# Sixteen weight slots, each at its own remainder modulo 256 bytes

## The chip, the core and the metric

One core of one Trainium2 chip runs the whole kernel. The metric is the device time of one execution in microseconds; the median of the runs shown counts. Five engines matter: TensorE (PE, and its weight loads PEld), VectorE (DVE), ScalarE (ACT), GpSimd (POOL) and the queue of SyncE (SP) that issues most DMAs. SBUF is the on-chip memory of 128 partitions; an address below is a byte offset within a partition, and a tile of 512 float32 columns takes 2048 bytes of each.

## The reference

One decoder block on x of 1024 rows by 1024 columns, float32:

```python
h    = rms_norm(x, norm1_g)
proj = h @ w_in                      # 1024 x 3584: retention q,k,v,gate; differential q,k,v
ret  = rms_norm(retention_chunkwise(rotary(rq), rotary(rk), rv)) * silu(rg)   # 8 heads of 64
dif  = rms_norm((softmax(q1 k1') - lam * softmax(q2 k2')) v) * (1 - LAMBDA_INIT)  # 4 heads of 128, causal
x    = x + concat([ret, dif]) @ w_out
h2   = rms_norm(x, norm2_g)
x    = x + (silu(h2 @ w_gate) * (h2 @ w_up)) @ w_down     # 2816 wide
```

## The kernel before

**Three matmuls for one.** Every large product is made to float32 accuracy from the faster type float32r: each operand is split into a high part (a rounded copy, made by ScalarE, or by a scaled activation) and a low part (the operand minus its high part, by VectorE). `mm3` then issues high-high, high-low and low-high into the same PSUM bank. So TensorE runs triples of matmuls, 512 columns wide (384 in the differential head groups), each with its own load of a stationary block of 128 columns (512 bytes).

**The weight slots.** The pool `wp` holds eight slots for high parts (tag `whi`), eight for low parts (tag `wlo`) and two raw pages (`raw`), in that order. A slot is a tile of 512 float32r columns. The list `slot` names the first eight pairs, which the planned part of the kernel reuses by hand; later, `Strassen.weights` and `operand` take new tiles of the same two tags, which the pool hands out in turn over the same places. The slots hold, in order of time:

- in the differential stage (0 to about 235 us) the 384 columns of w_in of head groups 0 and 2 (`w_chunk`, `w_parts`), streamed against stationary blocks of the transposed x (`hT`). Groups 1 and 3 use `dslot`, another pool on the right side of SBUF with tags of the same names, which the change does not touch;
- in the seven products P1 to P7 of the retention projection, twice (to about 470 us), the weights (`prepare`, `halves_`, `product`), streamed against `hT`, `sx` and `sb`;
- in the output projection (`o_proj`) the transposed mixture as stationary blocks (`mix_turn`), and in its second half four of w_out's blocks as streams (`wo_part`);
- in the gate and up products (about 555 to 950 us), seven products for each pair of column blocks, weights as stationary blocks (`first_weights`, `Strassen.weights`), with the normalised x (`blk`, tiles elsewhere) streamed;
- in the down product (950 us to the end) both sides: `operand` makes the slot pair of an activation block (stationary) and the next pair for the weights (streamed).

**What lies where.** On the left side of SBUF the constants come first, then the pools `act`, `wp`, `st`, `rowa` and those opened later (`dif`, `sx`, `sbp`, `ap`); on the right `edge` (one tile of 24 columns that nothing reads), `wd`, later `prp`. Behind the constants and `edge`, rows of tiles are multiples of 256 bytes.

**Order.** Up to the gate and up products the instructions are planned: each is added with an engine, an estimated duration and the names of what it reads and writes (`Plan.add`), the plan assigns times (`Plan.times`), and the instructions are issued in that order. From there on the loops issue them in program order. Neither looks at an address. Two lines make and hand out the slots:

```python
    slot = [[wp.tile([P, 512], F32R, tag=tag, name=tag) for tag in ("whi", "wlo")] for _ in range(KC)]
    ...
        hi, lo = (wp.tile([P, 512], F32R, tag=tag_, name=tag_) for tag_ in ("whi", "wlo"))
```

Of the kernel before, what the change touches and what calls it, by code (L numbers as in the profile page):

```python
# [11 lines left out]
F32R = mybir.dt.float32r  # L12
# [4 lines left out]
P = 128  # L17
# [3 lines left out]
KC = D // P  # L21
# [9 lines left out]
NP = 5  # L31
NAT = 4
WARM = 2


C_ID = 0
# [36 lines left out]
def block_kernel(ctx: ExitStack, tc: tile.TileContext, x, norm1_g, w_in, ret_norm_g, dq_g, dk_g,  # L73
# [39 lines left out]
    wp = ctx.enter_context(tc.tile_pool(name="wp", bufs=KC))  # L113
# [190 lines left out]

    late = {}
    hT = [[act.tile([P, 4, 2, 4, P], F32R, tag="act", name="act") for _ in range(2)] for _ in range(2)]
    slot = [[wp.tile([P, 512], F32R, tag=tag, name=tag) for tag in ("whi", "wlo")] for _ in range(KC)]
    rawk = [(f"raw{i}", wp.tile([P, 512], F32, tag="raw", name="raw", bufs=NRAW)) for i in range(2)]
    mixd = [rowa.tile([P, 512], F32, tag="rowa", name="rowa") for _ in range(NT)]
    rowk = [(f"ra{i}", mixd[i]) for i in range(NT)]  # L310
# [54 lines left out]
    V.memset(zero, 0.0)  # L365
    for _ in range(WARM):
        T.matmul(bank[0], zero[:, :P], zero, start=True, stop=True)
# [383 lines left out]
    for s in range(ND + 3):  # L751
# [10 lines left out]
        if s < ND:  # L762
            g, k = s // NT + 1, s % NT
# [654 lines left out]
    class Strassen:  # L1418
# [10 lines left out]
        def weights(self, n):  # L1429
            (i, j), other, op, *_ = PRODUCTS[n]  # L1430
            src = self.raw[j][:, :, i, :]
            if other is not None:
                both = wp.tile([P, 512], F32, tag="raw", name="sum", bufs=NRAW).rearrange("p (k e) -> p k e", e=P)
                G.tensor_tensor(out=both, in0=src, in1=self.raw[other[1]][:, :, other[0], :], op=op)
                src = both
            hi, lo = (wp.tile([P, 512], F32R, tag=tag_, name=tag_).rearrange("p (k e) -> p k e", e=P)
                      for tag_ in ("whi", "wlo"))
            A.copy(hi, src)
            self.w[n] = hi, lo
            V.tensor_tensor(out=lo, in0=src, in1=hi.bitcast(F32), op=ALU.subtract)  # L1440
# [45 lines left out]
    at = {}  # L1486
# [42 lines left out]


    def operand(x_, y_=None, op=None):
        hi, lo = (wp.tile([P, 512], F32R, tag=tag_, name=tag_) for tag_ in ("whi", "wlo"))
        if y_ is not None:
            both = wp.tile([P, 512], F32, tag="raw", name="sum", bufs=NRAW)
            G.tensor_tensor(out=both, in0=x_, in1=y_, op=op)
            x_ = both
        A.copy(hi, x_)
        V.tensor_tensor(out=lo, in0=x_, in1=hi.bitcast(F32), op=ALU.subtract)
        return hi, lo
# [3 lines left out]
    for n, (_, (b0, b1, bop), outs, done) in enumerate(DOWN):  # L1543
        m = [bankh() for _ in range(4)] if n % 2 == 0 else [bankp(), bankp(), bankm([P, 512]), bankm([P, 512])]
        for c in range(NH):
            b = [w_get(c, *name) for name in (b0, b1) if name is not None]
            i = n * NH + c
            ah, al = operand(ring[i % len(ring)])
            if i + len(ring) < 7 * NH:
                a_load(i + len(ring))  # L1550
            bh, bl = operand(*b, bop) if bop else operand(*b)
            if i in LAST:
                plane(LAST[i], NH - 1)

            if n < len(STARTS) and c < 4:
                for sh, dh in STARTS[n]:
                    t = 4 * sh + c
                    acc[t][dh] = (rowa if dh else prp).tile([P, 512], F32, tag="rowa" if dh else "pr", name="acc")
                    SY.dma_start(acc[t][dh], x2d[t * P:(t + 1) * P, dh * 512:(dh + 1) * 512])
            for t in range(4):  # L1560
                mm3(m[t], ah[:, t * P:(t + 1) * P], al[:, t * P:(t + 1) * P], bh, bl, c == 0, c == NH - 1)
        for t in range(4):
            for (sh, dh), sign in outs.items():
                o = acc[4 * sh + t][dh]
                V.tensor_tensor(out=o, in0=o, in1=m[t], op=ALU.add if sign > 0 else ALU.subtract)
                if (sh, dh) in done:
                    row = (4 * sh + t) * P
                    SY.dma_start(out[0, row:row + P, dh * 512:(dh + 1) * 512], o)
# [25 lines left out]
```

## Time and profile before

| what | before |
|---|---|
| median of 2 runs (lowest, highest) | 1180.64 us (1179.64, 1181.64) |
| profiled execution: its own time, its span | 1179.49 us, 1177.7 us |
| granted TensorE clock, mean | 0.999 |
| PE busy | 1169.5 us, 5872 matmuls |
| PE weight loads busy | 1004.7 us |
| DVE, ACT, POOL busy | 895.4, 604.5, 506.5 us |
| matmuls of 512 columns that read a slot, mean duration of one | 389 to 401 ns |

The profile is of one execution, whose own time is 1.8 us longer than the span from its first to its last instruction. All instructions of this kernel are recorded under one line of the source (a helper's, L101), so groups are told apart by the names of the tiles they write and read, out<-in, with buffer numbers left out. Durations of matmuls overlap (one of 512 columns lasts 389 ns while the next starts after some 227 ns), so the pace is read from start to start.

### The profile page before, as it was taken

The page shows a single profiled execution, that of the slowest core. Times are in us where ns is not written, and L with a number is a line of the kernel's source. Part 1 is how long each engine was busy: PE and PEld are TensorE (multiplying, and loading weights), DVE is VectorE, ACT ScalarE, POOL GpSimd, SP SyncE. Part 2 cuts the span into 40 slices and gives each one's busy share as a digit, 9 for nine tenths or more (in the row PEclk, how much of TensorE's full clock was granted, in tenths as well). Part 3 has the DMA queues.
Part 4 walks back from the last instruction along what each step waited for, and adds up shares of the span by engine and source line. Part 5 has one row for each costly group of instructions (what it writes and reads, how often), then busy time and mean ns, then how long its engine had stood idle before and what let it go on. Part 6 is the DMA issues. An engine that isn't in the chain of part 4 may idle for free.

```text
span 1177.7 us, 17427 instructions
## 1 busy us (share of the span) xinstructions
PE 1169.5 (99%) x5872; PEld 1004.7 (85%) x5872; DVE 895.4 (76%) x1561; ACT 604.5 (51%) x1332; POOL 506.5 (43%) x581
## 2 busy tenths in 40 slices
PE   9999999999999999999999999999999999999998
PEld 7999999988888888888888888888888888888887
DVE  6988888888779866758987756666665769698696
ACT  7767566666366745836444343434344334344442
POOL 4668786510012111301276654565456535263153
PEclk9999999999999999999999999999999999999999
DMA  7278776537644862322133423332323388933341
GB/s 213 69 173 150 136 115 117 162 124 235 223 126 148 266 201 90 95 88 90 58 131 117 134 76 98 111 119 90 99 99 116 106 293 265 354 101 90 98 138 67
DMA packets 118009, 164.29 MB, mean 139 GB/s; under 512 B 11936, under 2 KB 62240, under 8 KB 117792
## 3 DMA queue, kind: packets, MB, share of 16 engines
q1 hardware_dynamic: 110976, 152.62, 39.4%
q0 software_dynamic: 5760, 10.49, 6.5%
q8 instruction: 46, 0.75, 0.3%
q14 instruction: 43, 0.35, 0.1%
q10 hardware_dynamic: 1184, 0.07, 0.1%
HBM read 110.97 MB, written 54.26 MB: 140 GB/s over the span
## 4 chain that ended last, share of the span: by engine, by line
PE 93%; DVE 4%; ACT 2%; issue 1%; DMA 1%; SPq 0%; POOL 0%; DVEq 0%; ACTq 0%
PE h L101 39%; PE pp L101 31%; PE m L101 19%; PE big L101 4%; ACT pr L101 1%; DVE wx L101 1%; DVE wy L101 1%; DVE wlo L101 1%; DMA spare<-in_w_in_dram 1%; DVE pr L101 0%; DVE rowa L101 0%; DVE sx L101 0%; ACT wy L101 0%; DVE acc L101 0%; ACT whi L101 0%
## 5 line engine op out<-in xcount | busy, mean ns | idle before, releaser
L101 POOL TENSOR_TENSOR sum<-rawp 128x512 f32<-128x512 f32 x100 | 141.8, 1419 | 175.0 <-DVE wlo L101 144.9
L101 ACT CAST whi<-sum 128x512 fp32r<-128x512 f32 x155 | 96.4, 622 | 197.8 <-PE h L101 58.7
L101 DVE TENSOR_TENSOR wlo<-sum,whi 128x512 fp32r<-128x512 f32 x155 | 158.6, 1024 | 34.4 <-ACT whi L101 34.2
L101 PE MATMUL pp<-whi,act 128*128 128x384 f32 (+1 forms) x592 | 180.9, 359 | 0.2 <-DVE qkn L101 0.2
L101 POOL TENSOR_TENSOR sum<-wide 128x512 f32<-128x512 f32 x55 | 85.7, 1560 | 128.5 <-DVE wlo L101 101.8
L101 PEld LDWEIGHTS pp<-whi,act 128*128 128x128 f32 x592 | 109.4, 188 | 4.9 <-ACT q L101 0.6
L101 PE MATMUL h<-sx,whi 128*128 128x512 f32 x360 | 111.3, 390 | 0.0
L101 DVE TENSOR_TENSOR wlo<-wide,whi 128x512 fp32r<-128x512 f32 x99 | 77.5, 805 | 33.2 <-ACT whi L101 33.2
L101 ACT CAST whi<-wide 128x512 fp32r<-128x512 f32 x99 | 59.3, 621 | 84.2 <-PE m L101 43.3
L101 PE MATMUL pp<-wlo,act 128*128 128x384 f32 (+1 forms) x296 | 102.5, 346 | 0.0
L101 PEld LDWEIGHTS h<-sx,whi 128*128 128x128 f32 x360 | 67.2, 188 | 13.7
L101 DVE TENSOR_TENSOR wlo<-rawp,whi 128x512 fp32r<-128x512 f32 x44 | 48.6, 1105 | 38.6 <-ACT whi L101 37.7
L101 PE MATMUL h<-whi 128*128 128x512 f32 x196 | 76.7, 391 | 0.0
L101 DVE TENSOR_TENSOR c<-c,h 128x512 f32<-128x512 f32 x80 | 52.9, 681 | 31.3 <-PE h L101 31.3
L101 PE MATMUL h<-whi,wlo 128*128 128x512 f32 x196 | 76.3, 389 | 0.0
L101 PE MATMUL h<-wlo,whi 128*128 128x512 f32 x196 | 76.3, 389 | 0.0
L101 POOL TENSOR_TENSOR fsum<-c 128x512 f32<-128x512 f32 x50 | 70.7, 1426 | 8.1 <-DMA ffd<-fsum 8.1
L101 PE MATMUL h<-sx,wlo 128*128 128x512 f32 x180 | 70.1, 389 | 0.0
L101 POOL TENSOR_TENSOR stt<-stt,cs 128x1 f32<-128x1 f32 (+1 forms) x64 | 57.9, 906 | 3.7
L101 PEld LDWEIGHTS pp<-wlo,act 128*128 128x128 f32 x296 | 55.9, 189 | 1.9
L101 DVE CUSTOM_DVE_ANT_0 big<-big,zm 128x128 f32<-128x128 f32 (+7 forms) x64 | 47.7, 771 | 8.8 <-PE big L101 8.6
L101 PE MATMUL h<-b,whi 128*128 128x512 f32 x176 | 54.3, 390 | 0.0
(328 smaller groups left out, 3136.4 us busy)
## 6 DMA issues: line engine op xcount, KB each, us to landing
wide<-ffd SPq DMA_DIRECT2D x77, 256.0 KB, 2.7
ffd<-fsum SPq DMA_DIRECT2D x55, 256.0 KB, 2.0
rawp<-in_w_gate_dram SPq DMA_DIRECT2D x22, 512.0 KB, 3.5
rawp<-in_w_up_dram SPq DMA_DIRECT2D x22, 512.0 KB, 3.6
wide<-in_w_down_dram SPq DMA_DIRECT2D x44, 256.0 KB, 5.4
sumd<-act POOLq DMA_DIRECT2D x40, 256.0 KB, 4.2
rowa<-cd SPq DMA_DIRECT2D x32, 256.0 KB, 2.9
cd<-pr SPq DMA_DIRECT2D x24, 256.0 KB, 2.8
```

The source lines that it names most:

```text
L101: i = getattr(self.engine, op)(*(now(a) for a in args), **{k: now(a) for k, a in kw.items()})
```

## The change

The row of a slot's tile grows from 512 to 520 elements (2080 bytes, which is 8 x 256 + 32), and the slot is a view of 512 of them: from the first element on for high parts, from the fifth (16 bytes on) for low parts. So the eight slots of each tag lie 32 bytes apart modulo 256, and all sixteen begin at different remainders. The three places that took such tiles now take the view. Instructions, their shapes and their order stay.

```diff
+SKEW = {"whi": 0, "wlo": 4}
...
-    slot = [[wp.tile([P, 512], F32R, tag=tag, name=tag) for tag in ("whi", "wlo")] for _ in range(KC)]
+    def spaced(tag):
+        at = SKEW[tag]
+        return wp.tile([P, 520], F32R, tag=tag, name=tag)[:, at:at + 512]
+
+    slot = [[spaced(tag) for tag in ("whi", "wlo")] for _ in range(KC)]
...
-            hi, lo = (wp.tile([P, 512], F32R, tag=tag_, name=tag_).rearrange("p (k e) -> p k e", e=P)
+            hi, lo = (spaced(tag_).rearrange("p (k e) -> p k e", e=P)
                       for tag_ in ("whi", "wlo"))
...
-        hi, lo = (wp.tile([P, 512], F32R, tag=tag_, name=tag_) for tag_ in ("whi", "wlo"))
+        hi, lo = (spaced(tag_) for tag_ in ("whi", "wlo"))
```

## The prediction

> **What bounds the kernel now.** I read the page's share of engines and its chain first, then the same span cut by stage.
>
> ```profile
> PE 1169.5 (99%) x5872; PEld 1004.7 (85%) x5872; DVE 895.4 (76%) x1561; ACT 604.5 (51%) x1332; POOL 506.5 (43%) x581
> ...
> PE 93%; DVE 4%; ACT 2%; issue 1%; DMA 1%; SPq 0%; POOL 0%; DVEq 0%; ACTq 0%
> ```
>
> TensorE is busy for 99% of the span and holds 93% of the chain that ended last. Only something that changes TensorE's pace, or starves it, can move the time. The stages say the same:
>
> ```profile
> 0.00:235.00 235.00, 231.92 (x1476) 221.64 (x1477) 193.28 (x544) 159.40 (x442) 154.24 (x287) 1.00 0.64 142
> 235.00:470.00 235.00, 234.56 (x1204) 198.80 (x1202) 186.72 (x331) 137.85 (x316) 29.74 (x53) 1.00 0.54 176
> 470.00:560.00 90.00, 89.38 (x491) 76.46 (x491) 63.34 (x108) 57.43 (x146) 17.58 (x32) 1.00 0.29 92
> 560.00:950.00 390.00, 390.00 (x1723) 322.92 (x1722) 266.65 (x367) 158.94 (x274) 210.62 (x150) 1.00 0.31 104
> 950.00:1178.00 228.00, 223.65 (x987) 184.87 (x985) 185.39 (x214) 90.85 (x156) 94.34 (x60) 1.00 0.53 178
> ```
>
> The columns are the stretch, its length, then busy time with count for PE, weight loads, VectorE, ScalarE and GpSimd, the granted clock and the DMA share. The clock is 1.00 throughout, so it is no lever. From 560 us on, TensorE is covered almost without a hole; VectorE, next in line, has 228.0 - 185.4 = 42.6 us free in the last stage.
>
> A matmul's "busy" is modelled, so the pace has to come from start to start. The chain in order of time gives it (start, length, what, how many matmuls):
>
> ```profile
> 33.11 3.13 PE pp L101 x18
> ...
> 261.20 5.44 PE h L101 x24
> ...
> 1083.89 29.92 PE h L101 x132
> ```
>
> 5.44 / 24 and 29.92 / 132 are both 226.7 ns for a matmul of 512 columns. At 33 us they are 384 columns wide: 3.13 / 18 = 173.9 ns. So 128 columns cost 52.8 ns, 0.4125 ns each, and 512 columns would be 211.2 ns: **about 15.5 ns of each matmul do not depend on its width**. That the pace is so even, whatever VectorE, ScalarE and the DMAs are doing, is the most useful fact here: accesses of other engines to the weight slots do not reach TensorE.
>
> It is not even everywhere. Just after a break (transposes, waits) the starts are uneven for a while:
>
> ```profile
> 243.78 0.40 PE L101 MATMUL big<-kl,qz 128*128 128x512 f32 x1
> 244.01 0.40 PE L101 MATMUL big<-kh,q 128*128 128x512 f32 x1
> 244.25 0.39 PE L101 MATMUL big<-kl,qz 128*128 128x512 f32 x1
> 244.47 0.39 PE L101 MATMUL big<-kh,q 128*128 128x512 f32 x1
> 244.70 0.40 PE L101 MATMUL big<-kl,qz 128*128 128x512 f32 x1
> 244.94 0.39 PE L101 MATMUL big<-kh,q 128*128 128x512 f32 x1
> 245.16 0.39 PE L101 MATMUL big<-kl,qz 128*128 128x512 f32 x1
> ```
>
> The steps are 0.23, 0.24, 0.22, 0.23, 0.24, 0.22: between about 220 and 240 ns, in the mean (245.16 - 243.78) / 6 = 230 ns, with no semaphore to wait for between them. The same matmuls then settle at 226.7 ns and stay. So the pace depends on some phase between the streams that TensorE reads, and in long runs it finds one that repeats. This is where an address could matter.
>
> **The change, part by part.** No instruction, DMA, wait or queue position is added, removed or moved: the hand-written order comes from names and estimated durations, which the addresses do not enter. What moves are addresses. Before, the tiles behind the constants have rows that are multiples of 256 bytes, so all operands of the wide matmuls have one remainder modulo 256. After it, slot i of the eight stands 32 i bytes further, and the low parts 16 more: sixteen slots, sixteen remainders. Each pool of eight slots grows by 8 x 32 = 256 bytes, so what lies behind keeps its remainder, and nothing else changes its place against the others.
>
> How many matmuls read a slot? The tile views of the two names, cut by stage, give 528 + 550 + 230 + 1149 + 966 = 3423 with a high part and 264 + 281 + 125 + 574 + 637 = 1881 with a low part:
>
> ```profile
> 0.00:235.00 235.00, 158.23 (x528) 97.27 (x528) 24.97 (x40) 25.04 (x40) 1.00 0.64 142
> 235.00:470.00 235.00, 176.18 (x550) 102.66 (x550) 41.64 (x60) 38.36 (x60) 1.00 0.54 176
> 470.00:560.00 90.00, 65.58 (x230) 41.01 (x231) 12.15 (x18) 11.18 (x19) 1.00 0.29 92
> 560.00:950.00 390.00, 352.95 (x1149) 215.37 (x1148) 128.20 (x144) 88.65 (x143) 1.00 0.31 104
> 950.00:1178.00 228.00, 222.30 (x966) 180.93 (x964) 149.72 (x154) 89.76 (x154) 1.00 0.53 178
> ```
>
> ```profile
> 0.00:235.00 235.00, 89.30 (x264) 49.93 (x264) 24.97 (x40) 1.00 0.64 142
> 235.00:470.00 235.00, 107.57 (x281) 52.87 (x281) 41.64 (x60) 1.00 0.54 176
> 470.00:560.00 90.00, 44.08 (x125) 23.51 (x125) 12.15 (x18) 1.00 0.29 92
> 560.00:950.00 390.00, 223.19 (x574) 107.55 (x574) 128.20 (x144) 1.00 0.31 104
> 950.00:1178.00 228.00, 197.72 (x637) 119.55 (x637) 149.72 (x154) 1.00 0.53 178
> ```
>
> Those that read one of each are counted twice:
>
> ```profile
> L101 PE MATMUL h<-whi,wlo 128*128 128x512 f32 x196 | 76.3, 389 | 0.0
> L101 PE MATMUL h<-wlo,whi 128*128 128x512 f32 x196 | 76.3, 389 | 0.0
> ...
> L101 PE MATMUL pp<-wlo,whi 128*128 128x512 f32 x78 | 30.3, 389 | 0.0
> ...
> L101 PE MATMUL pp<-whi,wlo 128*128 128x512 f32 x78 | 30.3, 389 | 0.0
> ...
> L101 PE MATMUL m<-wlo,whi 128*128 128x512 f32 x66 | 25.7, 389 | 0.0
> L101 PE MATMUL m<-whi,wlo 128*128 128x512 f32 x66 | 25.7, 389 | 0.0
> ```
>
> 2 x (196 + 78 + 66) = 680. Of the rest, two head groups (1 and 3) read slots of another pool under the same names, 2 x 8 x 8 x 3 = 384. That leaves 3423 + 1881 - 680 - 384 = **4240 matmuls** of 5872 whose reads move, nearly all of them 512 wide. Each nanosecond per matmul is 4.2 us.
>
> The cost of one moved read is not in the trace: every wide matmul had the same remainder. It is bounded by the steps above. From below: the shortest, about 224 ns within the 10 ns that the rows resolve, 2.7 less than the settled 226.7: -11 us; and, if the whole width-independent part could vanish, -15.5 x 4240 = -66 us. From above: the longest, about 236 ns, at every one of them: +9.3 x 4240 = +39 us. **I take nothing**, which is nearest to the rows: the pace of the last three stages is the same for matmuls that load slots (560 to 950 us, where the slots are the stationary or moving side of all) and for those that stream them, and the same for 384 and 512 columns but for the width.
>
> The Trainium skill ("SBUF — State Buffer", section "Who interferes with whom") speaks against any effect: TensorE has a read port each for the streamed operand and for weight loads, and waits on nobody. By that rule the sum is exactly 0. The trace agrees for other engines (the even 226.7 ns) but its uneven steps after breaks show that TensorE's own pace is not one constant, and no run so far has two remainders to compare.
>
> Writes and reads of the slots by ScalarE and VectorE:
>
> ```profile
> L101 ACT CAST whi<-sum x155: 603/623/627, 576.6 to 1163.9; 128x512 fp32r<-128x512 f32 x155
> L101 DVE TENSOR_TENSOR wlo<-sum,whi x155: 675/691/1787, 581.3 to 1164.9; 128x512 fp32r<-128x512 f32 x155
> ```
>
> Minimum, median and maximum. ScalarE's spread is 24 ns; VectorE's long ones coincide with GpSimd at work and have nothing to do with a remainder that all shared. If a shifted slot cost each 24 ns, that would be about 300 x 24 = 7 us on each engine, beside TensorE, which is not waiting for them: in the six rows of two slots above its idle time is 0.0. If that cover went, TensorE would wait for low parts in the last stage, where VectorE has those 42.6 us free. I cost it at 0.
>
> The sum: 1179.49 (the profiled execution, span 1177.7 and 1.8 around it) + 0 = 1179.5; the median of the two runs is 1.2 above that, so **1180.6**, with 4 us either way for runs and small shifts.
>
> **The rivals.**
>
> 1. *The repeat is lost* (other side: slower). If the phase that long runs settle in depends on equal remainders, the three matmuls of a triple (high-high, high-low, low-high) now follow each other with unequal ones and the pace stays that of the uneven stretches. Price: 230 - 226.7 = 3.3 ns, 14 us at all 4240 and 7 us at half; with 20 ns of rounding in the 1.38 us it may be 19 us. Time 1187 to 1199. It decides from the first long run, at 257 us; earlier, transposes break the runs anyway. For it: the steps of 220 to 240 ns without a wait. Against it: a phase may belong to when instructions are issued, not to where they read.
> 2. *The new remainders collide.* As 1, but most matmuls take the longest step: 24 to 39 us, 1204 to 1220. For it: such steps exist. Against: in the rows they alternate with short ones.
> 3. *A better phase*, the short steps more often than now: 3 to 11 us less, 1169 to 1177.
> 4. *Equal remainders are what costs the 15.5 ns.* All operands begin on one remainder, so weight load and stream could get in each other's way at every matmul, and spreading them would end it. Between a third and all of 66 us: 1114 to 1157; TensorE would then stand at about 213 us in the last stage, still above VectorE's 185. For it: the fixed part is there and unexplained. Against: a collision of two streams would hardly cost the same at 384 and 512 columns. The Trainium skill ("TensorE: Matmul & The Clock Gate", section "Wait — 56ns, not 53.3ns?") has 215.7 ns for 512 warm columns, measured back to back; by that 11.0 ns of the 226.7 are excess, 47 us over these matmuls, an estimate that gives 1134. The trace does not show that pace for any wide matmul of this kind.
> 5. *The change does not do what it says*: if rows of 520 elements were rounded up, the spacing would vanish and only the 16 bytes remain. It ends like my forecast and is held in it.
>
> **How the numbers follow.** Forecast 0.44 (1176 to 1185), rival 1 0.26, rival 3 0.10, rival 2 0.12, rival 4 0.08. Within 2% of 1180.6 lie 1157 to 1204 (2% is about what a measurement of this kernel can tell from no change): the first three cases, 0.80; faster 0.08; slower 0.12. The range of 1168 to 1200 takes in the forecast, rival 1 and rival 3.
>
> **What would show it.** The chain's groups of 24 matmuls stay at 5.44 us if I am right; 5.5 or more is rival 1, 5.6 and up rival 2, 5.4 and less rival 3 or 4. The stretch from 560 to 950 us, where the slots meet tiles that did not move, and the last one, where both sides are slots, should then differ, since their remainders do. I am wrong if these groups change; if they do not but the time does, it is a wait of TensorE for a low part, and the idle time before those six groups would be above zero.

## The result, and the profile after

The changed kernel takes 1199.39 us (1198.34 to 1200.44), against 1180.64 before: 18.75 us more, a ratio of 1.0163 with a 95% interval of 1.0146 to 1.0180. That is the upper end of rival 1 (1187 to 1199), not the forecast of no change.

The page of the changed kernel (its profiled span is 1198.6 us), the same parts as before:

```profile
PE 1190.5 (99%) x5872; PEld 1007.0 (84%) x5872; DVE 886.8 (74%) x1561; ACT 605.1 (50%) x1332; POOL 507.7 (42%) x581
...
PE 95%; DVE 2%; ACT 2%; DMA 0%; issue 0%; POOL 0%; SPq 0%; DVEq 0%; ACTq 0%
```

The counts are the same, the clock too, and the other engines' busy time is within 9 us of what it was. TensorE holds more of the chain, and the 21 us are all in its own row: it is busy longer with the same matmuls. The chain in order of time says where (start, length, what, how many matmuls). Before:

```profile
257.10 4.09 PE pp L101 x18
...
561.65 10.88 PE h L101 x48
...
964.21 29.92 PE h L101 x132
...
1143.73 27.89 PE h L101 x123
```

and after:

```profile
34.84 3.15 PE pp L102 x18
...
259.25 4.19 PE pp L102 x18
263.44 5.56 PE h L102 x24
...
567.82 11.16 PE h L102 x48
...
980.51 30.58 PE h L102 x132
...
1164.00 28.50 PE h L102 x123
```

The four rows of before are the same matmuls as those at 259.25, 567.82, 980.51 and 1164.00 us after. The delay is 2.15 us at the first, 6.17 at the second, 16.30 at the third and 20.88 at the end of the last (1192.50 against 1171.62). So the long runs of wide matmuls pay: 4.0 us in the retention products and the output projection, 10.1 in the gate and up products, 4.6 in the down product. The differential stage pays next to nothing by its pace (3.15 / 18 = 175 ns, 173.9 before: 0.02 us in this group). Of its 2.15 us, 1.73 stand before the first row (34.84 against 33.11), and a kernel below, with everything moved together, shows the same delay without any loss of time. A group of 48 takes 232.5 ns each in place of 226.7, one of 132 takes 231.7.

The two-slot groups and the writers of the slots, in the views shown before:

```profile
L102 PE MATMUL h<-whi,wlo 128*128 128x512 f32 x196 | 77.3, 394 | 0.0
L102 PE MATMUL h<-wlo,whi 128*128 128x512 f32 x196 | 76.8, 392 | 0.0
```

```profile
L102 ACT CAST whi<-sum x155: 602/622/627, 582.9 to 1183.8; 128x512 fp32r<-128x512 f32 x155
L102 DVE TENSOR_TENSOR wlo<-sum,whi x155: 677/686/1789, 588.0 to 1184.8; 128x512 fp32r<-128x512 f32 x155
```

TensorE does not wait before these groups (0.0), their mean duration is 3 to 5 ns up from 389, and the engines that write the slots take as long as before (medians of 622 and 686 ns, 623 and 691 before). What remains is the pace of TensorE with nobody in its way.

### The profile page after: what moved, and what is told of

It reads as the page before. It is cut to its first block, busy times and chain, and to the rows that moved or that the text cites. A ratio compares the mean times of both kernels' runs of the same rounds, so it can differ in the third digit from the quotient of the medians.

```text
span 1198.6 us, 17427 instructions
## 1 busy us (share of the span) xinstructions
PE 1190.5 (99%) x5872; PEld 1007.0 (84%) x5872; DVE 886.8 (74%) x1561; ACT 605.1 (50%) x1332; POOL 507.7 (42%) x581
## 4 chain that ended last, share of the span: by engine, by line
PE 95%; DVE 2%; ACT 2%; DMA 0%; issue 0%; POOL 0%; SPq 0%; DVEq 0%; ACTq 0%
PE h L102 40%; PE pp L102 32%; PE m L102 19%; PE big L102 4%; ACT pr L102 1%; ACT wy L102 0%; DMA rowa<-cd 0%; DVE wlo L102 0%; DVE wx L102 0%; POOL stt L102 0%; DVE acc L102 0%; ACT whi L102 0%; DVE wy L102 0%; DVE pr L102 0%; SPq L102 0%
## 5 line engine op out<-in xcount | busy, mean ns | idle before, releaser
L102 DVE TENSOR_TENSOR wlo<-sum,whi 128x512 fp32r<-128x512 f32 x155 | 149.4, 964 | 34.7 <-ACT whi L102 34.4
```

What stands on the lines that cost most here:

```text
L102: i = getattr(self.engine, op)(*(now(a) for a in args), **{k: now(a) for k, a in kw.items()})
```

## The experiments

Four theories stood for why. **A**: a run of matmuls settles (its steps from start to start become even) only while those that follow each other begin at equal remainders. **B**: it is the distance modulo 256 between the stationary and the streamed operand that costs. **C**: only the 16 bytes matter. **D**: only the old remainder itself is fast. In the changed kernel and in the first four experiments every engine issues the same instructions with the same waits as before; the sweeps and the last two kernels differ in some waits, so there the pace of unbroken stretches is read and not the time.

### One half of the change at a time, and one common shift

```diff
-SKEW = {"whi": 0, "wlo": 4}
+SKEW = {"whi": 0, "wlo": 0}          # spacing only, rows of 520
```

> Rows of 520 elements, but low parts not shifted: the eight slots of a tag lie 32 bytes apart modulo 256, the high and low part of a pair are equal. Theory A (lost repeat: the pace settles only while the matmuls that follow each other have operands at the same remainders): within the 12 matmuls of a gate or up product all slot operands are equal and only the next product starts elsewhere, so part of the settling comes back: 1186 to 1195 us, groups of 12 in the gate and up stage between 2.72 and 2.79 us. Theory B (a certain distance between stationary and streamed operand costs, whatever comes before): the seven of eight slots that are away from the streamed tiles stay slow, 1196 to 1200 us. Theory C (only the 16-byte shift of low parts matters): back to 1181 us.

Measured: 1200.15 us, ratio 1.0163 (1.0148 to 1.0178). The expectation was wrong on one point of fact: in the down product the pool hands out slots in the order in which they come free, so high and low parts of a pair are often not neighbours and their remainders differ there. In the gate and up stage they are equal, and there it can be read.

```diff
     # rows of 512, low slots 32 bytes on
+    his = [wp.tile([P, 512], F32R, tag="whi", ...) for _ in range(KC)]
+    wp.tile([P, 8], F32R, tag="pad1", ...)
     ... the eight "wlo" tiles
+    wp.tile([P, 56], F32R, tag="pad2", ...)
```

> Rows of 512 elements as before; all low slots 32 bytes further on, high slots where they were, pages behind in place. Only two remainders. Theory A: high and low follow each other in every triple, so the repeat is broken everywhere the slots are used: 1192 to 1200 us, unless a pattern of three repeats by itself, which would show as one fixed length for all groups of 24 matmuls. Theory B: only the third of the matmuls that load or stream a low part is slow: +5.4 ns at some 1400, 1187 to 1190 us. Theory C: 1181 if only distances that are no multiple of 32 matter.

Measured: 1201.84 us, ratio 1.0178 (1.0161 to 1.0195). That is just beyond A's 1192 to 1200 and far from B's 1187 to 1190: moving the low slots alone costs as much as the whole change. The sweep of the low parts, below, comes back to this.

```diff
+    wp.tile([P, 8], F32R, tag="pad0", ...)    # all sixteen slots 32 bytes on
     ... eight "whi" tiles, eight "wlo" tiles, rows of 512
+    wp.tile([P, 56], F32R, tag="pad2", ...)
```

> Rows of 512 elements; all sixteen slots 32 bytes further on than before, pages behind in place. One remainder for all slots, another for all other tiles. Theory A: what follows each other is equal again, so long runs settle: 1180 to 1184 us, 5.44 us for 24 matmuls in the last stage and one fixed length in the gate and up stage. Theory B: gate and up products, where slots meet tiles elsewhere, stay at 5.55 to 5.60 us for 24; the last stage, where both sides are slots, is back at 29.92 us for 132: 1190 to 1195 us. Theory D (slots are fast only at their old remainder): slow everywhere, 1196 to 1200 us.

Measured: 1197.03 us, ratio 1.0139 (1.0124 to 1.0154). Its chain, first in the retention products and the gate and up stage, then in the down product:

```profile
264.85 5.60 PE h L102 x24
270.45 2.80 PE pp L102 x12
...
569.32 11.20 PE h L102 x48
...
983.72 29.93 PE h L102 x132
1043.57 29.92 PE h L102 x132
1103.41 29.92 PE h L102 x132
```

This run tells the theories apart. Where slots meet tiles elsewhere, now 32 bytes away from them, each matmul takes 5.60 / 24 = 11.20 / 48 = 233.3 ns, at the same length group after group: the run has settled, at a slower pace. Where both sides are slots, at equal remainders again but 32 bytes from the old one, it is 29.92 / 132 = 226.7 ns, exactly as before. A falls as the whole cause (settled and slow), D falls (another remainder and fast), and so do C's 1181 us for the spacing and for the low shift. B has the groups right, and 2 us too little in the whole (1190 to 1195). The chain with the spacing alone agrees in the main:

```profile
919.27 2.75 PE pp L102 x12
...
952.65 2.80 PE pp L102 x12
955.45 2.80 PE h L102 x12
...
977.74 30.74 PE h L102 x132
1039.21 30.73 PE h L102 x132
```

All 12 matmuls of a product are at one distance. At most distances a product takes 2.79 or 2.80 us, 233 ns each, though within it nothing changes. Only at distance 0, one product in eight (the first row), and at 192 bytes does it take 2.75 us, 229 ns each. Even that is more than the 2.72 us of the kernel before, where the product ahead has the same remainder; the last experiment shows why.

### Everything moved together

```diff
-    edge = ctx.enter_context(... .tile([P, 24], F32, name="edge")
+    edge = ctx.enter_context(... .tile([P, 16], F32, name="edge")
+    ctx.enter_context(tc.tile_pool(name="pad", bufs=1)).tile([P, 8], F32, name="pad")
     act = ctx.enter_context(tc.tile_pool(name="act", bufs=4))
```

> The kernel before, with every tile but the constants moved by 32 bytes modulo 256 (a pad of 32 bytes behind the constants on the left, the first tile on the right 32 bytes shorter). All wide matmuls again have stationary and streamed operand at one remainder, but another one than before. If the distance between the two operands decides (theory B as the runs so far leave it): 1179 to 1183 us, 5.44 us for 24 matmuls. If the remainder itself decides (theory D): 1196 to 1202 us. The identity for the transposes stays behind by 32 bytes; if distances cost transposes too, some 460 of them would add up to 2 us.

Measured: 1180.16 us, ratio 0.9996 (0.9986 to 1.0006). Its chain:

```profile
263.22 5.44 PE h L101 x24
...
563.52 10.88 PE h L101 x48
...
1025.92 29.92 PE h L101 x132
```

The old pace to the digit, at a remainder of 160 instead of 128. The first of these rows comes 2 us later than before too (the same matmuls as at 261.20 there), with no loss in the median: the delay at the beginning of a profiled execution is not the change's.

### Which distances cost

```diff
+    slots_in = {tag: wp.tile([P, KC * 512 + 64], F32R, tag=tag, bufs=1, ...) for tag in ("whi", "wlo")}
+    def spaced(tag, at=0):             # `at` set per pair of column blocks, and per product
+        n = next_slot[tag] % KC * 512 + at
+        next_slot[tag] += 1
+        return slots_in[tag][:, n:n + 512]
```

> The slots are views of one row of 8 x 512 + 64 elements per part, so that they can be moved by any number of bytes while the kernel runs. In the gate and up stage high and low parts are both moved by 256, 4, 8, 16, 32, 48, 64, 96, 128, 192 bytes for the ten pairs of column blocks after the first; in the down stage the streamed parts by 256, 16, 32, 48, 64, 128, 192 for its seven products, the stationary ones not. Waits differ a little from before, so only the pace within runs of matmuls counts. Theory A: 226.7 ns for every move, since inside a block pair all is equal (a settled pace may be another one for some moves, but a fixed one). Theory B: 226.7 at 256 bytes and at multiples of some period, 230 to 236 elsewhere; the moves at which it comes back give the period.

> The sweep again, with other moves: in the gate and up stage 144, 160, 172, 176, 180, 184, 188, 196, 200, 252 bytes, in the down stage the streamed parts by 256, 8, 4, 60, 72, 80, 96 bytes. In the first sweep the pace was 227.2 ns at a distance of 256 bytes, 229.0 at 192 and 230.7 to 234.2 elsewhere. Theory B with one best distance: all of these stay above 226.7. If 192 is the flank of a dip, one of its neighbours is at or under 226.7, which would point to a faster version.

In the gate and up stage TensorE stays busy all but without a break in these kernels (the stretches at 4 bytes alone have waits, which are left out of the mean), so the matmuls counted in 36 us give the pace. The first sweep at 256, 16, 32 and 192 bytes, in that order (stretch, length, PE busy and matmuls, clock, DMA):

```profile
586.00:622.00 36.00, 36.00 (x159) 1.00 0.35 111
...
704.00:740.00 36.00, 36.00 (x156) 1.00 0.28 90
744.00:780.00 36.00, 36.00 (x156) 1.00 0.30 97
...
940.00:976.00 36.00, 36.00 (x159) 1.00 0.64 213
```

The mean step from start to start in the trace is finer. Distance in bytes by which the stationary slots were ahead, and ns for a matmul of 512 columns:

| bytes | 256 | 4 | 8 | 16 | 32 | 48 | 64 | 96 | 128 | 144 |
|---|---|---|---|---|---|---|---|---|---|---|
| ns | 227.2 | 232.4 | 230.7 | 233.3 | 233.3 | 233.3 | 233.3 | 234.2 | 232.4 | 233.3 |

| bytes | 160 | 172 | 176 | 180 | 184 | 188 | 192 | 196 | 200 | 252 |
|---|---|---|---|---|---|---|---|---|---|---|
| ns | 233.3 | 235.6 | 230.1 | 233.3 | 232.0 | 233.2 | 229.0 | 233.3 | 230.7 | 233.4 |

256 bytes count as none; every other distance tried here costs between 1.8 and 8.4 ns, and none is faster than equal remainders. The low value at 192 has no lower one beside it. In the down stage, with the streamed side moved, runs are broken by waits in these kernels, and the uneven steps after each wait raise the mean; there 60 bytes gave 227.1 ns, against 229.1 at 256, and all others 229.6 to 236.2. At 60 bytes the steps settle on 227, 226, 227, exactly as at no distance, so there this distance costs nothing. Counted as in the table it is 196, which cost some 6 ns in the gate and up stage. This is not explained: equal remainders were always fast in settled runs, but the rule that all else is slow has this one exception.

> The sweep with low parts alone moved, high parts left at the remainder of the streamed tiles: 256, 4, 8, 16, 32, 64, 96, 128, 192, 224 bytes in the gate and up stage, and the streamed low parts by 256, 16, 32, 64, 128, 192, 224 in the down stage. If each matmul pays for its own distance, a third of the matmuls pay and the mean is 226.7 plus a third of what the first sweep showed (228 to 229 ns). If one unequal member of a triple keeps the whole run from settling (what is left of theory A; the run with low parts 32 bytes on had 238.7, 228 and 232 ns in turn), the mean is 231 to 234 ns as with both parts moved.

Measured, mean per matmul of a triple in the gate and up stage: 233.1 at 4 bytes, 231.1 at 8, 232.2 at 16, 233.3 at 32, 231.2 at 64, 232.6 at 96, and 231.1 at 128, 192 and 224. In the down stage, broken by waits, moving the streamed low parts alone gave 229.8 to 233.2, with 229.9 at 256 bytes. So one low part out of place among three costs as much as all three at 32 bytes, two thirds as much at 64 and more at 192: nowhere the third that each matmul paying for itself would give. This is what made halves of the change cost the whole. The run with the low shift alone shows such a triple (two high, one low) in the timeline:

```profile
800.06 0.63 PE L102 MATMUL pp<-sx,whi 128*128 128x512 f32 x2
800.53 0.39 PE L102 MATMUL pp<-sx,wlo 128*128 128x512 f32 x1
800.76 0.63 PE L102 MATMUL pp<-sx,whi 128*128 128x512 f32 x2
801.23 0.39 PE L102 MATMUL pp<-sx,wlo 128*128 128x512 f32 x1
801.46 0.63 PE L102 MATMUL pp<-sx,whi 128*128 128x512 f32 x2
```

A triple takes 0.70 us, again and again (3 x 226.7 would be 0.68).

### Whose distance

```diff
-                mm3(m[t], ah[...], al[...], bh, bl, c == 0, c == NH - 1)
+                T.matmul(m[t], a_, bh, start=c == 0, stop=False)
+                T.matmul(m[t], l_, bl, start=False, stop=False)
+                T.matmul(m[t], a_, bh, start=False, stop=c == NH - 1)
```

> Low slots 32 bytes on, as in the run with the low shift alone, and in the down product the three matmuls of a triple are high-high, low-low, high-high in place of high-high, high-low, low-high (the cross terms are left out there: it is a timing experiment). Each matmul now has its own stationary and streamed operand at one remainder, while the weights loaded during it are at another one in two of three. In the run with the low shift it was the other way round (weights loaded during a matmul always at the remainder of its stream, its own weights not in two of three) and the pace of that stage was 232.2 ns. If a matmul's own pair decides: 226.7 to 228 ns in the down stage. If what is loaded during it decides as well, or any change of remainder from one matmul to the next: 231 to 234 ns.

Measured, in the down product (the whole took 1200.52 us):

```profile
980.12 30.64 PE h L102 x132
1041.42 30.65 PE h L102 x132
1102.72 30.65 PE h L102 x132
```

232.1 ns. With the low shift alone each matmul of that product streams at the remainder of the weights that are loaded during it; here it streams at the remainder of its own. Either alone is not enough: in these runs a stretch is fast where all that TensorE reads for neighbouring matmuls lies at one remainder. In both, the remainder also changes from matmul to matmul, and they cannot tell what that costs from what a distance costs.

```diff
+            ah, al = operand((8 * (c % 8),) * 2, ring[i % len(ring)])
+            bh, bl = operand((8 * (c % 8),) * 2, *b, ...)      # both sides moved together, 0 to 224 bytes
```

> Slots as views of one row of 8 x 512 + 64 elements per part, as in the sweeps; everything at the old remainder, but in the down product both sides of a block of 12 matmuls are moved together, by 0, 32, 64 ... 224 bytes in turn. Within a block stationary and streamed operands are equal, and the remainder of both changes every 12 matmuls. Waits differ from the kernel before, so only steps below 300 ns count; the sweeps' stretch at a distance of 256 bytes had 229.1 ns in this stage. If the distance decides: 229 to 230 ns. If each change of remainder throws the matmuls out of step for some ten of them, as a break does: 231 to 233 ns.

Measured: 229.0 to 229.4 ns at each of the eight remainders, the step across a change not counted; the sweep had 229.1 at 256 bytes in that stage. TensorE waits in this kernel, so its time of 1199.3 us says nothing here. The two means agree, but that does not show that a change is free: the sweep's holds the uneven steps after waits. One product here runs through without a wait:

```profile
1032.87 30.29 PE h L103 x132
```

30.29 / 132 = 229.5 ns, where the kernel before has 29.92 us and 226.7 ns for a product without a wait. The starts in the trace show where the rest goes. At each change comes one step of 235 ns, then seven uneven ones (230, 224, 231, 236, 228, 233 and 231 ns or nearly so), then 227, 226, 227 until the next change. So a change costs some 34 ns, 2.8 ns a matmul when it comes every 12, even where both sides make it together; in between, the run settles on the same 226.7 ns at each of the eight remainders. The second expectation had the mechanism, and a size too large. The 2.75 us at distance 0 in the kernel with the spacing alone are the same: 30 ns over 2.72.

## Why the prediction was wrong

**What bounds the kernel** held: the loss is all in TensorE's pace, with no wait behind it; ScalarE, VectorE and the DMAs play no part, and their term of 0 was right. The count of matmuls was right too, but not all of them pay: the differential stage, whose runs are short and broken by transposes, keeps its pace.

**The step that failed is the cost of one moved read, "I take nothing".** The runs showed 5.0 to 5.8 ns a matmul in its place, in the long groups of wide matmuls. The argument for it was that all stages have one pace. But all stages had it because all operands lay at one remainder; evenness where nothing varies says nothing of what happens when it does. The uneven steps of 220 to 240 ns after a break, which the text itself read as a phase between the streams, were the row nearest to the new state, and their mean (230 ns) was the better value. The chances followed that choice: 0.44 for no change, 0.26 for what came nearest. The 2% that the prediction took for the limit of a measurement was too wide as well: the interval here is 0.17% either way.

**Rival 1 had the sign and the place, and a price too small.** It took 3.3 ns at 4240 matmuls, 14 us. Its upper end of 19 us does not follow from its 20 ns of rounding: over six steps these are 3.3 ns more, up to 28 us in all. That the result lies at that upper end is therefore in part luck. The runs show 5.8 ns in groups of 48 and 5.0 in groups of 132, 18.7 us of chain from 257 us on; the start of the loss was as written. Its mechanism was half right. A change of remainder does break the repeat, at some 34 ns each. But a run at one unequal distance, with nothing to change, settles and is as slow: 233.3 ns at 32 bytes. How the two share the loss of the changed kernel, where distances and changes come together, no run separates.

**Rival 2** began at 24 us, 5.7 ns at all 4240; the loss is 18.7 us. Of single distances, only 172 bytes comes near its longest step (235.6 ns). **Rivals 3 and 4** (a better phase, or the fixed part as the price of equal remainders) are refuted: of 19 distances none in the gate and up stage beats equal remainders. The part of a matmul that does not depend on its width was read 2 ns too large: the group at 33 us has uneven steps at its head, and its later ones are 173.3 ns, which leaves 13.3 in place of 15.5. No run here touched these. **Rival 5**: the spacing took effect, since the spacing alone costs as much as the change.

The Trainium skill's rule ("SBUF — State Buffer", section "Who interferes with whom": TensorE waits on nobody) gave 0. For other engines the rows agree: settled groups of 24 and of 132 keep 226.7 ns in the kernel before, whatever the others do. The Trainium skill ("TensorE: Matmul & The Clock Gate", section "Step-by-step: what each phase is for") adds that loading the next weights takes no read bandwidth from the running matmul. With all slots 32 bytes on, 233.3 against 226.7 ns by the distance of the two addresses alone shows that the pace of these float32r matmuls is not independent of where the two lie. Here the measurement decides. Whether the two reads meet in the memory, and in which part of it, no run shows.

## What to carry to other kernels

When float32r matmuls with a weight load each set the pace, keep stationary and streamed operands at the same remainder modulo 256 bytes: pad a pool or a constant by a few bytes rather than give each slot its own, and do not change the remainder from product to product. A row length that is not a multiple of 256 bytes can cost 3% of every matmul in it with no instruction changed and no wait to be seen; look at the length of a settled group in the chain, not at engine shares. And a number that is the same everywhere is no bound for a case in which its common cause is taken away.

## What the runs showed of the hardware that was not expected

- The pace of a matmul depends on the distance of its operands' addresses modulo 256 bytes: 226.7 ns at 0, 229.0 to 235.6 at 19 other distances in the gate and up stage, for 512 columns of float32r with a weight load each. In the down stage one distance (60 bytes on the streamed side) settled on 226.7 too.
- One operand in three out of place can cost as much as all three (233.3 ns at 32 bytes for either).
- A change of remainder costs some 34 ns, spread over eight steps, even when both operands make it together.
- Settled paces come in fixed lengths: triples of 0.68 or 0.70 us in the rows above. In the trace of the kernel before, twelve settled runs of 10 to 2716 steps, begun after different waits, have all their starts on one grid of 6.67 ns, but for a slow drift. What makes this grid is open; 226.7 and 233.3 are 34 and 35 of its steps.
